# First group of two chunk pairs ahead of the second group in both MLP up stages, own memory for its tiles, weight block sums two pairs late

## The chip, the core and the metric

The kernel runs on one core of a Trainium2 chip. The core has a matrix engine (TensorE, "PE" in the profile, with its weight loads as "PEld"), a vector engine (VectorE, "DVE"), a scalar engine (ScalarE, "ACT"), GpSimd ("POOL") and a sync engine ("SP"), which here issues all transfers between HBM and the on-chip memory. Each engine works through a queue of its own in a fixed order and waits for others by semaphores. The metric is device time in microseconds (us) of one execution; lower is better.

## What is computed

The reference is a network of two layers over 256 context tokens and 1024 latent tokens of width 1024: a gated convolution mixer in the first layer, an mLSTM mixer in the second, each followed by a dense MLP with squared ReLU and a hidden width of 4096. All of it is in float32. The change touches the MLP alone:

```python
def _sqrelu_mlp(h, w1, w2):
    return jnp.square(jax.nn.relu(h @ w1)) @ w2

...
        x = x + mx[2] * _rmsnorm(yx, nw[1])
        x = x + mx[5] * _rmsnorm(_sqrelu_mlp(_modulate(_rmsnorm(x, nw[2]), mx[3], mx[4]), mlp_w1[i], mlp_w2[i]), nw[3])
```

## The kernel before, in words

**Products.** Each float32 matrix is split into a rounded part and its remainder (a cast on ACT, a subtraction on DVE), and a product is three passes over the parts. Both MLP products are done blockwise: the operands are cut into 2 x 2 blocks, and seven products of sums of blocks take the place of eight block products. The sums over token blocks are made once (`sums`, `pre_norm2`, L313 to L351), those over weight blocks for each chunk pair.

**MLP up, `mlp_up` (L484).** The hidden width makes 32 chunks of 128, taken as NQ = 16 chunk pairs. `up_weights` (L401) loads two chunks of w1 into `raw` tiles (a ring of three buffers of 4 KB, L406), makes three difference blocks (two of them into `tw` tiles, two buffers), and splits seven pieces into a ring of eight slots. `up_group` (L427) multiplies them with one group of tokens: seven products of twelve matmuls into four accumulators X, Y, Z, W, some of them filled twice, with ACT and DVE taking sums out on the way into a store tile `st` (L439, tag `st7`, seven blocks), whose last line stores it to `hid_d` in HBM (L465). There are two token groups, A0 (384 of 640 half tokens in layer 0, 256 of 512 in layer 1) and A1 (256). `down_sums` (L467) loads the two chunks of w2 that belong to a pair, makes four differences and stores them to `t_d`, which `mlp_down` reads later.

**Order around the start.** `out_proj` ends with the last token tiles; what fills A0 is done inside it, and the last two token pairs are left as two functions in `left`, each of which makes one half of A1: four steps of four transposes, two copies on ACT into a `val` tile, four sums on DVE into an `S` tile, and two splits into A1 (L326 to L351; `val` and `S` share one tag, two buffers). Before: pair 0 with A0, then `left`, then pair 0 with A1, the block sums of pair 0, then pairs 1 to 15 with A0 and A1 each and their block sums behind them; in the last pair A1 comes first.

**MLP down, `mlp_down` (L503).** Seven products one after the other, each over 16 pairs: a piece of w2 or `t_d` (`w_piece`, through `raw` and the ring) and a piece of `hid_d` (`h_piece`: loaded into `hr`, three buffers, L521; split into `hp`, four buffers, L522 and L523), both prefetched. Sums go to four quarter tiles in the pool Y.

**Memory and order.** Pools are stacks at the left and the right end of the on-chip memory, and a pool opened on bytes of a closed one waits, tile by tile, for the last user of what lay there. Before, the store tiles and `tw` lie in M0 and M on the right, M0 where the post-norm tiles T of `out_proj` were; A1 is the lowest pool on the left in the up stage, H the lowest in the down stage, and Y lies on the right. A list scheduler sets the fixed order of each queue: of the instructions that it deems ready, the one that comes first in the program.

## Time and profile before

| | |
|---|---|
| median of the runs | 2597.91 us (3 runs, 2596.24 to 2599.75) |
| profiled execution | 2592.09 us, span 2590.3 us |
| PE busy | 2489.9 us, 96% of the span |
| DVE busy | 1640.9 us, 63% |
| ACT busy | 1139.0 us, 44% |
| MLP up of layer 0 | 528.03 to 950.61 us of the span |
| MLP up of layer 1 | 1921.42 to 2269.56 us |
| mean granted PE clock | 0.986 of full speed |

One execution was recorded by the hardware profiler. Times in its rows are microseconds from the start of the span. A row of the timeline joins neighbouring instructions of one line; its bracket says how long the engine stood idle before it and what ended that. Matmul ends are modelled, so the start of the next row is the better end of a group.

### The profile page before, as it was taken

What the parts mean: (1) busy time and instruction counts of PE and PEld (TensorE: products, weight loads), DVE (VectorE), ACT (ScalarE), POOL (GpSimd) and SP (SyncE); (2) the same over time, 40 slices, a digit from 0 to 9 for tenths busy, and PEclk for the clock granted to TensorE, in tenths of its full rate; (3) what the DMA queues carried; (4) which work ended last, traced back from release to release, by engine and by line L of the source; (5) the groups of instructions that cost most, each with busy time, mean ns of one, the idle gap of its engine ahead of it and who ended that gap; (6) DMA issues with size and microseconds to landing.
All of it is one profiled execution on the core that took longest, in us unless ns stands there. A gap on an engine that the chain in (4) does not pass through costs nothing.

```text
span 2590.3 us, 38783 instructions
## 1 busy us (share of the span) xinstructions
PE 2489.9 (96%) x14520; PEld 2202.5 (85%) x14520; DVE 1640.9 (63%) x3036; ACT 1139.0 (44%) x2489; POOL 104.8 (4%) x229
## 2 busy tenths in 40 slices
PE   8999999979999999999999899999998999999998
PEld 6888887879999998888879788887778999988887
DVE  5777885676766754445863755546467877754565
ACT  6311113554454544334654434345455555544443
POOL 1000000100000000000111100000010000000010
PEclk9999999989999999999999999999998999999999
DMA  8456663426656675555751322222426777776575
GB/s 294 131 176 192 204 191 111 154 98 238 238 209 228 219 252 177 169 170 169 236 175 57 73 78 58 67 73 61 150 99 213 251 261 252 234 248 190 183 228 186
DMA packets 229631, 452.77 MB, mean 175 GB/s; under 512 B 17738, under 2 KB 109178, under 8 KB 229442
## 3 DMA queue, kind: packets, MB, share of 16 engines
q1 hardware_dynamic: 229442, 450.29, 53.5%
q8 instruction: 114, 1.87, 0.3%
q14 instruction: 75, 0.61, 0.1%
HBM read 324.68 MB, written 125.33 MB: 174 GB/s over the span
## 4 chain that ended last, share of the span: by engine, by line
PE 53%; issue 30%; DVE 7%; DMA 6%; ACT 2%; POOL 2%; SPq 0%; DVEq 0%; POOLq 0%; ACTq 0%
PE psd L528 11%; PE op L371 5%; PE psZ L429 4%; PE psW L429 4%; PE psX L429 4%; PE psv L857 3%; PE psc L129 3%; PE pso L129 3%; PE psb L129 3%; PE psu L129 3%; DMA Dm<-nm_d 3%; PE psY L429 2%; DMA mraw<-in_mod_w_dram 2%; PE psq L129 1%; POOL rstd L242 1%
## 5 line engine op out<-in xcount | busy, mean ns | idle before, releaser
L528 PE MATMUL psd<-w,hp 128*128 128x512 f32 x3024 | 705.0, 395 | 0.0
L528 PEld LDWEIGHTS psd<-w,hp 128*128 128x128 f32 x3024 | 569.1, 188 | 132.0
L523 DVE TENSOR_TENSOR hp<-hr,hp 128x512 fp32r<-128x512 f32 (+1 forms) x226 | 169.5, 752 | 254.9 <-ACT hp L522 254.5
L522 ACT CAST hp<-hr 128x512 fp32r<-128x512 f32 (+1 forms) x226 | 151.1, 669 | 325.5 <-PE psd L528 291.4
L123 DVE TENSOR_TENSOR w<-raw,w 128x512 fp32r<-128x512 f32 x384 | 261.7, 686 | 37.2 <-ACT w L122 36.9
L122 ACT CAST w<-raw 128x512 fp32r<-128x512 f32 x384 | 236.5, 617 | 94.8 <-DMA raw<-in_w_dram 29.6
L429 PE MATMUL psX<-A,w 128*128 128x256 f32 (+1 forms) x1536 | 233.4, 300 | 4.9 <-ACT st L444 3.7
L429 PE MATMUL psZ<-A,w 128*128 128x256 f32 (+1 forms) x1536 | 230.9, 298 | 0.2 <-DVE st L448 0.2
L429 PE MATMUL psW<-A,w 128*128 128x256 f32 (+1 forms) x1536 | 228.1, 296 | 0.0
L429 PEld LDWEIGHTS psX<-A,w 128*128 128x128 f32 x1536 | 216.7, 192 | 6.0 <-ACT st L444 4.0
L429 PEld LDWEIGHTS psZ<-A,w 128*128 128x128 f32 x1536 | 215.4, 190 | 0.6 <-DVE st L448 0.4
L429 PEld LDWEIGHTS psW<-A,w 128*128 128x128 f32 x1536 | 213.0, 189 | 0.2 <-DVE st L450 0.2
L371 PE MATMUL op<-w,zs 128*128 128x512 f32 x864 | 205.7, 397 | 6.5 <-ACT zs L365 4.4
L371 PEld LDWEIGHTS op<-w,zs 128*128 128x128 f32 x864 | 162.2, 190 | 43.6 <-ACT zs L365 5.4
L459 ACT ACTIVATE st<-st 128x256 f32<-128x256 f32 (+1 forms) x192 | 85.3, 444 | 249.1 <-DVE st L450 181.9
L220 DVE SCALAR_TENSOR_TENSOR macc<-mraw,sil,macc 128x1024 f32<-128x1024 f32 x112 | 140.6, 1282 | 37.4 <-DMA mraw<-in_mod_w_dram 37.0
L109 ACT CAST w<-raw 128x1024 fp32r<-128x1024 f32 (+1 forms) x73 | 75.4, 1041 | 161.7 <-PE psc L129 60.4
L110 DVE TENSOR_TENSOR w<-raw,w 128x1024 fp32r<-128x1024 f32 (+1 forms) x73 | 87.8, 1210 | 80.1 <-ACT w L109 79.0
L857 PE MATMUL psv<-w,hT 128*128 128x256 f32 (+1 forms) x960 | 133.8, 293 | 1.1 <-ACT val L270 0.9
L429 PE MATMUL psY<-A,w 128*128 128x256 f32 (+1 forms) x768 | 121.6, 305 | 12.8 <-ACT w L122 11.6
L857 PEld LDWEIGHTS psv<-w,hT 128*128 128x128 f32 x960 | 123.7, 192 | 1.9 <-ACT val L270 1.2
L429 PEld LDWEIGHTS psY<-A,w 128*128 128x128 f32 x768 | 111.2, 195 | 15.2 <-ACT w L122 12.4
(242 smaller groups left out, 3437.7 us busy)
## 6 DMA issues: line engine op xcount, KB each, us to landing
hid_d<-st SPq DMA_DIRECT2D x48, 896.0 KB, 5.8
mraw<-in_mod_w_dram SPq DMA_DIRECT2D x80, 512.0 KB, 4.0
hr<-hid_d SPq DMA_DIRECT2D x104, 320.0 KB, 4.2
raw<-in_w_dram SPq DMA_DIRECT2D x64, 512.0 KB, 4.4
rw<-in_w_dram SPq DMA_DIRECT2D x64, 512.0 KB, 5.4
raw<-t_d SPq DMA_DIRECT2D x128, 256.0 KB, 3.2
hr<-hid_d SPq DMA_DIRECT2D x122, 256.0 KB, 2.8
raw<-in_w_dram SPq DMA_DIRECT2D x96, 256.0 KB, 3.9
```

The source lines that it names most:

```text
L110: nc.vector.tensor_sub(w[1], src, w[0].bitcast(F32))
L122: nc.scalar.copy(w[:, 0], src)
L123: nc.vector.tensor_sub(w[:, 1], src, w[:, 0].bitcast(F32))
L129: nc.tensor.matmul(ps, w[a][:, k * P : (k + 1) * P], hold["hT"][:, k, b, t0 : t0 + n], start=(k == 0 and i == 0), stop=(k == KD - 1 and i ...
L220: nc.vector.scalar_tensor_tensor(ac[v], raw, s, ac[v], ALU.mult, ALU.add)
L371: nc.tensor.matmul(ps[h], zs[:, a, k, :], ws[k][b][:, h * 512 : (h + 1) * 512], start=(k == 0 and i == 0), stop=(k == KD - 1 and i == 2),)
L429: nc.tensor.matmul(ps, w[i][:, a, k * P : (k + 1) * P], A[:, PIECE[i], b, k, :], start=(first and k == 0 and j == 0), stop=(k == 3 and j = ...
L459: nc.scalar.activation(c, c, AF.Relu)
L522: nc.scalar.copy(h[:, 0], r)
L523: nc.vector.tensor_sub(h[:, 1], r, h[:, 0].bitcast(F32))
L528: nc.tensor.matmul(ps, h[:, a, o : o + P], w[:, b], start=(first and j == 0), stop=(last and j == 2))
L857: nc.tensor.matmul(ps[:, 0 : self.g], hold["hT"][:, k, a_, t * P : (t + 1) * P], self.wv[k // self.per][b_][:, k % self.per * self.g : (k ...
```

## The change

Each `mlp_up` now takes group A0 of pairs 0 and 1 first, with `left` traced between the two, then group A1 of pair 1, and then makes the pieces of pair 0 a second time for its group A1. From pair 2 on both groups follow each other, A0 first, in the last pair too. The block sums of pair q come after the weights of pair q + 2; those of the last two pairs stand at the end. The store tile of A0 lies in a pool of its own on the left (S1, S3) with one buffer, that of A1 in M with one buffer; M itself goes from two buffers to one. The difference tiles of the first two pairs come from the `raw` ring. The `val` and `S` tiles of `left` get three buffers in layer 0 and four in layer 1. In the down stage Y moves from the right to the left, below H.

```diff
--- before.py
+++ after.py
@@ -325,7 +325,7 @@

         def rest(A, c0, pl, tag, m):
             for k0 in range(0, 4, m):
-                val, S = [pl.tile([P, 4, m, P], F32, tag=tag, name=nm) for nm in ("val2", "S2")]
+                val, S = [pl.tile([P, 4, m, P], F32, tag=tag, name=nm, bufs=4 if l and m == 1 else 3) for nm in ("val2", "S2")]
                 for kk in range(m):
                     pt = tp.tile([P, 512], F32, tag="tp", name="pt2")
                     for j in range(2):
@@ -398,7 +398,7 @@

     NQ = DFF // P // 2

-    def up_weights(l, q, M):
+    def up_weights(l, q, M=None):

         raw = []
         for j in range(2):
@@ -406,7 +406,11 @@
             nc.sync.dma_start(r, w1[l, 2 * q + j])
             raw.append(r)
         (b11, b21), (b12, b22) = [(r[:, 0:512], r[:, 512:1024]) for r in raw]
-        t2, t3 = [M.tile([P, 512], F32, tag="tw", name="tw", bufs=2) for _ in range(2)]
+        if M is None:
+            tw = rawp.tile([P, 1024], F32, tag="raw", name="tw0")
+            t2, t3 = tw[:, 0:512], tw[:, 512:1024]
+        else:
+            t2, t3 = [M.tile([P, 512], F32, tag="tw", name="tw", bufs=2) for _ in range(2)]
         w = {1: piece(b11)}
         nc.vector.tensor_sub(t3, b22, b12)
         nc.vector.tensor_sub(b12, b12, b11)
@@ -420,7 +424,7 @@
         w[4] = piece(b21)
         return w

-    def up_group(l, q, w, A, n, c0, M, acc):
+    def up_group(l, q, w, A, n, c0, pl, acc):


         def prod(ps, i, first):
@@ -436,7 +440,7 @@
                     )

         bank = lambda nm: acc.tile([P, 512], F32, tag="acc", name=nm)[:, 0:n]
-        st = M.tile([P, 7, n], F32, tag="st7", name="st7")
+        st = pl.tile([P, 7, n], F32, tag="st7", name="st7", bufs=1)
         r11, r12, r22, c21, u2 = [st[:, i] for i in (0, 1, 2, 5, 6)]
         X, Y, Z, W = bank("psX"), bank("psY"), bank("psZ"), bank("psW")
         add = nc.vector.tensor_add
@@ -481,24 +485,28 @@
         nc.sync.dma_start(t_d[l, k, :, 2], b12)
         nc.sync.dma_start(t_d[l, k, :, 0:2], r[1].rearrange("p (a b) -> p a b", a=2))

-    def mlp_up(l, As, sX, left, acc):
+    def mlp_up(l, As, sX, left, S1, acc):
+

         (A0, n0), (A1, n1) = As
-        with pool("M0", bufs=1, side="right") as M:
+        w = up_weights(l, 0)
+        up_group(l, 0, w, A0, n0, 0, S1, acc)
+        w = up_weights(l, 1)
+        for f in left:
+            f(A1)
+        up_group(l, 1, w, A0, n0, 0, S1, acc)
+        sX.close()
+        with pool("M", bufs=1, side="right") as M:
+            up_group(l, 1, w, A1, n1, n0, M, acc)
             w = up_weights(l, 0, M)
-            up_group(l, 0, w, A0, n0, 0, M, acc)
-            for f in left:
-                f(A1)
-        sX.close()
-        with pool("M", bufs=2, side="right") as M:
             up_group(l, 0, w, A1, n1, n0, M, acc)
-            down_sums(l, 0, M)
-            for q in range(1, NQ):
+            for q in range(2, NQ):
                 w = up_weights(l, q, M)
-                both = [(A0, n0, 0), (A1, n1, n0)]
-                for A, n, c0 in both if q < NQ - 1 else both[::-1]:
-                    up_group(l, q, w, A, n, c0, M, acc)
-                down_sums(l, q, M)
+                down_sums(l, q - 2, M)
+                up_group(l, q, w, A0, n0, 0, S1, acc)
+                up_group(l, q, w, A1, n1, n0, M, acc)
+            down_sums(l, NQ - 2, M)
+            down_sums(l, NQ - 1, M)

     def mlp_down(l, pairs, xsrc, finish, T, H, Y, acc, G):

@@ -768,14 +776,14 @@
         sB.close()
         sT.close()
         set_ring()
-        with pool("A1", bufs=1) as pA1:
+        with pool("S1", bufs=1) as S1, pool("A1", bufs=1) as pA1:
             A1 = pA1.tile([P, 7, 2, 4, 256], F32R, name="A1")
-            mlp_up(0, ((A0, 384), (A1, 256)), sX, left, acc)
+            mlp_up(0, ((A0, 384), (A1, 256)), sX, left, S1, acc)
         sA.close()
     sH, sT = ExitStack(), ExitStack()
     new_hT(sH)
     T = sT.enter_context(pool("T1", bufs=2, side="right"))
-    with pool("H", bufs=1) as H, pool("Y", bufs=1, side="right") as Y:
+    with pool("Y", bufs=1) as Y, pool("H", bufs=1) as H:

         def finish(t, xt, tt):
             if t >= NCT:
@@ -1121,11 +1129,11 @@
     sG.close()
     sT.close()
     set_ring()
-    with pool("A3", bufs=1) as pA1:
+    with pool("S3", bufs=1) as S1, pool("A3", bufs=1) as pA1:
         A1 = pA1.tile([P, 7, 2, 4, 256], F32R, name="A3")
-        mlp_up(1, ((A0, 256), (A1, 256)), sX, left, acc)
+        mlp_up(1, ((A0, 256), (A1, 256)), sX, left, S1, acc)
     sA.close()
-    with pool("T3", bufs=2, side="right") as T, pool("H2", bufs=1) as H, pool("Y2", bufs=1, side="right") as Y:
+    with pool("T3", bufs=2, side="right") as T, pool("Y2", bufs=1) as Y, pool("H2", bufs=1) as H:

         def finish2(t, xt, tt):
             for h in range(2):
```

## Rows read from the trace of the kernel before

**Rows 1.** Timeline of PE (start, length, engine, line, tiles, count), end of layer 0's up stage
```profile
901.11 2.27 PE L429 MATMUL psX<-A,w 128*128 128x384 f32 x12
...
915.89 1.59 PE L429 MATMUL psX<-A,w 128*128 128x256 f32 x12
...
925.87 1.58 PE L429 MATMUL psX<-A,w 128*128 128x256 f32 x12
...
950.61 9.68 PE L528 MATMUL psd<-w,hp 128*128 128x512 f32 x41
```

**Rows 2.** Timeline of PE, start of layer 0's up stage
```profile
528.03 2.29 PE L429 MATMUL psX<-A,w 128*128 128x384 f32 x12
...
536.24 4.21 PE L429 MATMUL psX<-A,w 128*128 128x384 f32 x12 [3.72 <-ACT st L444]
...
551.30 1.04 PE L335 MATMUL pt<-ident,tt 128*128 128x128 f32 x8
...
604.09 2.27 PE L429 MATMUL psX<-A,w 128*128 128x384 f32 x12
```

**Rows 3.** Timeline of PE, start of layer 1's up stage
```profile
1921.42 1.61 PE L429 MATMUL psX<-A,w 128*128 128x256 f32 x12
...
1989.54 1.58 PE L429 MATMUL psX<-A,w 128*128 128x256 f32 x12
```

**Rows 4.** Waits of PE, 527 to 605 us (total us, times, longest)
```profile
PE pt L335 <- ACT val L338: 5.4, 3, 3.7
PE psY L429 <- ACT w L122: 4.7, 1, 4.7
PE psX L429 <- ACT st L444: 3.7, 1, 3.7
```

**Rows 5.** Waits of PE, 1920 to 2000 us
```profile
PE psY L429 <- ACT w L122: 6.8, 2, 5.4
PE pt L335 <- ACT val L338: 6.1, 3, 3.8
```

**Rows 6.** Busy: stretch, length, PE, PEld, DVE, ACT, POOL, PE clock, DMA, GB/s
```profile
528.00:604.00 76.00, 61.36 (x369) 58.57 (x368) 56.69 (x121) 42.13 (x89) 1.67 (x5) 0.87 0.43 146
1921.00:1990.00 69.00, 54.51 (x375) 52.29 (x374) 53.48 (x121) 40.76 (x89) 1.67 (x5) 0.83 0.43 145
```

**Rows 7.** Timeline of ACT, start and end of layer 0's up stage
```profile
535.71 0.48 ACT L444 COPY st<-psX 128x384 f32<-128x384 f32 x1 [1.73 <-DVE tt L387]
...
939.04 1.45 ACT L522 CAST hp<-hr 128x640 fp32r<-128x640 f32 x2
```

**Rows 8.** Timeline of DVE, start of the up stages of both layers
```profile
555.54 0.55 DVE L464 TENSOR_TENSOR st<-st 128x384 f32<-128x384 f32 x1
...
559.70 0.69 DVE L349 TENSOR_TENSOR A<-S,A 128x512 fp32r<-128x512 f32 x1 [0.69 <-ACT A L348]
...
562.67 0.69 DVE L349 TENSOR_TENSOR A<-S,A 128x512 fp32r<-128x512 f32 x1 [0.69 <-ACT A L348]
...
1917.93 1.89 DVE L123 TENSOR_TENSOR w<-raw,w 128x512 fp32r<-128x512 f32 x3
...
1945.84 0.42 DVE L463 TENSOR_TENSOR st<-st 128x256 f32<-128x256 f32 x1
1946.18 0.42 DVE L464 TENSOR_TENSOR st<-st 128x256 f32<-128x256 f32 x1
```

**Rows 9.** DMA: issues of the span by tile; stores of L465, 1990 to 2270 us
```profile
raw<-in_w_dram SPq DMA_DIRECT2D x64, 512.0 KB, 4.4
...
DMA to landing us min/median/max: 4.5/5.8/7.7
```

**Rows 10.** SP, end of layer 0's up stage: longest wait (925 to 945 us), issues
```profile
SPq L521 <- PE psW L429: 5.4, 1, 5.4
...
919.95 0.38 SPq L465 DMA_DIRECT2D hid_d<-st  x1
...
936.02 1.27 SPq L521 DMA_DIRECT2D hr<-hid_d  x3
```

## The prediction

> **What bounds the kernel now.** The first thing to read is TensorE's list of waits, because the change touches only the two MLP up stages. Inside the pairs TensorE runs without a pause: a group on A0 of layer 0 takes 915.89 - 901.11 = 14.78 us, a group of 256 columns 925.87 - 915.89 = 9.98 us, and the first down product (950.61) follows the last up group with no idle time in its bracket [rows 1]. So the middle of the stage can't be shortened by anything here, and what is left are its two ends.
>
> The start is where time is lost. The first four groups of layer 0 last from 528.03 to 604.09, 76.1 us [rows 2]. Their own work is 2 x 14.78 + 2 x 9.98 = 49.5 us and 32 transposes at 1.04 / 8 us each, 4.2 us [rows 1, 2]: 53.7 us, so 22.4 us are lost. In layer 1 it is 1989.54 - 1921.42 = 68.1 us against 4 x 9.98 + 4.2 = 44.1 us [rows 1, 3]: 24.0 us lost. The waits give the reasons. In layer 0 TensorE waits 5.4 us for ACT's copies of the transposes, 4.7 us for a weight split, 3.7 us for the first copy into the store tile; the other two groups are 0.7 us [rows 4]. In layer 1 it is 6.8 and 6.1 us, with 1.5 us of smaller ones [rows 5]. That makes 14.5 and 14.4 us. The rest, 7.9 and 9.6 us, is the lower clock after the pauses: twelve matmuls of 384 columns took 4.21 us at 536.24, after a pause of 3.72 us, and 2.28 us in the full stage [rows 1, 2], with a mean granted clock of 0.87 and 0.83 in the two stretches [rows 6], so part of the time was at 1.2 GHz. Layer 0 has three long pauses, so I price the clock at 7.9 / 3 = 2.6 us for each pause of three us or more.
>
> Each wait has a known cause. The copy at 535.71 had idled for DVE's L387 on the last tile [rows 7]: the store tile lay on memory of the post-norm tiles. The 4.7 us hang, as I read the code, on the split of a difference tile, whose two buffers are shared with the block sums of pair 0. The transposes wait because a step of four products has only two buffers for its val and S tiles: the last subtractions of two steps start 562.67 - 559.70 = 2.97 us apart, and in each DVE idles 0.69 us for ACT [rows 8]. VectorE itself is busy 56.7 of 76 us and 53.5 of 69 us [rows 6], so it is the next bound: what is saved in waits is saved only as far as VectorE has work to put there.
>
> **The change part by part.** *The start, layer 0.* The store tile lies in S1 and the difference tiles of the first two pairs in the raw ring, so nothing of them waits for the post-norm (what lay on S1's bytes, out_proj's ring slots for k = 4 and 5, was last read before 528), and the first group runs 528.03 to 542.8 without the 3.7 us. The 16 + 16 transposes come when it ends (in the kernel before, the second pair's eight at 551.30 also came only when a group was done [rows 2]). TensorE then has 4.2 + 14.78 us of ready work, the transposes and group (1, A0), up to 561.8. A1's path is longer: 1.0 us of transposes ahead of the first step [rows 2], eight steps, and what VectorE still owes the first group, five of nine evictions. An eviction of 256 columns occupies 1946.18 - 1945.84 = 0.34 us; at 384 columns it lasts 0.55 against 0.42 us, so I take 0.45 [rows 8]: 2.3 us. A step occupies VectorE 2.97 - 0.69 = 2.28 us. With three or four buffers the idle 0.69 can be filled by the next step; the bounds of a step are 2.28 us (all of it) and 2.97 us (none). I take 2.28, as other VectorE work is queued too and idle time is what the added buffers attack. So A1 is whole at 542.8 + 1.0 + 8 x 2.28 + 2.3 + 0.7 (last subtraction) = 565.0, and TensorE pauses 3.2 us, one clock price of 2.6. The two groups on A1 take 20.0 us. Beside them VectorE has the second set of pair 0's pieces, eleven operations at 1.89 / 3 = 0.6 us [rows 8], 6.6 us, and 9 x 0.34 = 3.1 us of evictions for every 9.98 us: it just fits, and I add 1.5 us for the lag (bounds 0 and 4, what is left of the first groups' evictions). End at 589.1 for 604.1: **15.0 us gained**.
>
> *The start, layer 1.* Group (0, A0) ends at 1931.4. Pair 1's raw tiles can be loaded when pair 0's are split, about 1922, and land 4.4 us later [rows 9]. From 1926.4 VectorE has 6.6 us of pieces, 3.1 us of evictions and 0.8 us of post-norm, done at 1936.9, beside TensorE's group. Then eight steps and 1.0 us: A1 is whole at 1956.1. TensorE has run out at 1931.4 + 4.2 + 9.98 = 1945.6, pays one clock price, then 20.0 us and 1.5 us lag: 1980.2 for 1989.5, **9.3 us gained**. Here VectorE is the bound and the earlier group only fills the wait.
>
> *Second set of pieces for pair 0.* Per layer two loads of 512 KB, seven casts, eleven VectorE operations. VectorE's 6.6 us are counted above; the casts lie on ACT, which is behind VectorE in both stretches (42.1 and 40.8 us busy [rows 6]); the loads pass on SP's queue ahead of pair 2's. If the cover of the A1 groups were gone they would cost 6.6 us per layer.
>
> *Block sums two pairs late.* The same loads, four subtractions and three stores per pair, moved on SP's queue past two pairs of weight loads and group stores; nothing reads them before the second down product. In the middle they cost nothing, as TensorE hides them there before and after; at the start they leave the difference buffers to the pieces (in the figures above); at the end two sets of sums remain instead of one. POOL has nothing moved past it.
>
> *One store tile for each group instead of two buffers.* The A0 store is issued 919.95 - 915.89 = 4.1 us after its group ends [rows 1, 10]; stores land after 4.5 to 7.7 us [rows 9], so the tile is free at 11.8 us at the latest. Its next write comes after the A1 group and one product, 9.98 + 2.11 = 12.1 us. I take 0 (bounds 0 and 2 us); a gain is excluded, since no store was waited for there. The Trainium skill speaks against this edit: "Trainium Kernel Development and Optimization", section Best Practices, asks for double buffers so that DMA overlaps compute. By the trace the other group is the second buffer; by the rule it would be the last rival below.
>
> *The end: A1 last, H above Y.* This edit has a price, and no row shows it directly. Before, A1's group came first in the last pair. Y now lies lowest on the left and H above it: in layer 0 Y takes 40 KB, so H spans 40 to 67.5 KB while A1 spans 10.5 to 66.5 KB; in layer 1 32 to 54 KB inside 7 to 63 KB. H waits for A1 whole: SP's wait before the first h load is 5.4 us on psW, the last product of A1's group, and the three loads were issued at 936.02, just as that group ended [rows 10], although hr's own bytes were last read by its first product. After the change A1's group is the very last. TensorE then has nothing until the first load lands and is cast: 939.04 + 0.73 - 936.02 = 3.75 us [rows 7, 10], and then a clock price of 2.6: 6.35 us a layer, **12.7 us lost** in both (bounds 3.4 + 1.9 with a smaller tile and the one row's clock loss, and 6 + 3.2 if the loads share the DMA engines with the sums).
>
> *Sum.* 15.0 + 9.3 - 12.7 = 11.6 us. The profiled execution took 2592.09 us (span 2590.3 and 1.8 around it) and would take 2580.5. It lies 5.8 us under the median of the runs, 2597.91; on that the forecast is **2586.3 us**, 0.45% faster. About 0.2%, 5.2 us, is what a measurement of this kernel can tell from no change.
>
> **Rivals.** *The hole at the end isn't there* (H placed or awaited otherwise): 2597.9 - 24.3 = 2573.6. For it: no row shows where H will lie, the KB come from the tile sizes in the code; against it stands the wait on psW.
> *The step keeps its chain.* If a step stays at 2.97 us, A1 comes 5.5 us later in each layer, the start gains 9.5 + 3.8 us and the end takes 12.7 of it: 2597.3, no change. For it: each step still goes ACT, VectorE, ACT, VectorE, with one more buffer in layer 0; against it: the idle 0.69 us is small and other work is there.
> *Slower: the first h loads queue behind the last block sums.* All of them go through SP's one queue, which itself waits (the 5.4 us above). If the h load stands there behind a store of pair 15's sums, it waits for their load, four subtractions and the store before it: 2.4 us and, priced as a raw tile of the same 512 KB, 4.4 us twice [rows 9], up to 11.2 us more a layer, 2586.3 + 22.4 = 2608.7. It decides from 5.8 us of extra wait a layer. For it: two sums are left for the end; against it: SP issued the h loads ahead of other work at 936.02.
> *Slower: the single store tile.* A store that lands later than 8 us delays the group's first copy, and from some 4 us more (three products of 1.4 us) TensorE too; each us beyond is paid in 28 pairs: 2614 for one. The rows' longest is 7.7.
>
> **How the numbers follow.** Forecast 0.50, own range 2580 to 2594 by the bounds; no hole 0.12; chain kept 0.20; sums in the way 0.12; single store tile 0.06. The range must reach down to the case without a hole and up over the kept chain, 2573 to 2600, and leaves out 0.18. Faster by over 0.2%: nine tenths of the forecast, the case without a hole and a little of the kept chain, 0.60. Slower: the last two and a little of the kept chain, 0.20. Within: 0.20.
>
> **What would show it.** Right: no wait of the first group for its copy; steps of A1 some 2.3 us apart; four groups done 61 us after the first psX in layer 0 and 59 us in layer 1; a TensorE pause of 3 to 5 us before the first psd matmul in both layers, with the h load on SP waiting for psW and the clock low after it. Wrong: TensorE seamless into psd, steps still 3 us apart, copies of psX waiting for a store, or new pauses in the middle of a stage.

## The result and the profile after

The changed kernel takes **2578.51 us** (median of 4 runs, 2577.89 to 2583.12) against 2597.07 us for the kernel before, run beside it: a ratio of **0.9926**, 95% interval 0.9909 to 0.9942. A second set of runs on another chip gave 0.9936 (0.9924 to 0.9948). That is 18.6 us by medians; 2586.3 us and 11.6 us were forecast. The profiled execution took 2577.89 us with a span of 2576.1 us; the forecast on that scale was 2580.5. The two spans, 2590.3 and 2576.1 us, differ by only 14.2 us: the profiled execution of the kernel before lies 5.0 us under its median, and the first up stage of the kernel after began 2.6 us later (530.65 against 528.03 us). That start lies between 526.9 and 531.9 us over all runs told of here, and nothing below is read from it.

The gain sits where the forecast had it, at the two ends of the two MLP up stages. The timeline of PE after, at the end of both up stages (columns as in [rows 1]):

```profile
934.83 1.58 PE L433 MATMUL psW<-A,w 128*128 128x256 f32 x12
940.87 49.44 PE L536 MATMUL psd<-w,hp 128*128 128x512 f32 x200 [4.45 <-ACT hp L530]
...
2242.80 1.58 PE L433 MATMUL psW<-A,w 128*128 128x256 f32 x12
2248.35 5.49 PE L536 MATMUL psd<-w,hp 128*128 128x512 f32 x12 [3.97 <-ACT hp L530]
2256.19 44.11 PE L536 MATMUL psd<-w,hp 128*128 128x512 f32 x182 [2.35 <-ACT hp L530]
```

Four lengths describe the run. The *work* of an up stage goes from the start of its first psX row to the end of its last psW row: in layer 0 it began at 530.65, so 934.83 + 1.58 - 530.65 = 405.8 us (422.7 before), in layer 1 at 1913.40, so 331.0 us (348.3 before). That is **17.0 and 17.3 us gained** where 15.0 and 9.3 were forecast. The *hole* is the time from there to the first psd row: 4.5 us in layer 0 and 4.0 us in layer 1, where before psd followed at once [rows 1]. The *middle* goes from layer 0's first psd row to layer 1's first psX row: 1913.40 - 940.87 = 972.5 us (970.8 before). The *tail* is the rest of the span: 2576.1 - 2248.35 = 327.8 us (320.7 before); it holds the second pause of 2.35 us in the rows above. All experiments below are read by these four. Each comes from one profiled execution, and two profiles of the changed kernel differ by up to 1.5 us in one of them, so differences of that size carry little by themselves.

At the start, the waits of PE from 528 to 605 us, to be set against [rows 4]:

```profile
PE pt L335 <- ACT val L338: 2.1, 1, 2.1
PE psX L433 <- ACT st L448: 0.6, 1, 0.6
PE psX L433 <- DVE w L123: 0.4, 1, 0.4
PE psZ L433 <- DVE st L452: 0.2, 1, 0.2
```

The first copy of 3.7 us and the weight split of 4.7 us are gone, and the transposes wait 2.1 instead of 5.4 us. In layer 1, 1912 to 1985 us, against [rows 5]:

```profile
PE pt L335 <- ACT val L338: 3.5, 3, 1.4
PE psX L433 <- ACT st L448: 1.1, 1, 1.1
```

The busy times of two stretches of the same lengths (columns as in [rows 6]) show that VectorE does more in the same time, 62.7 and 62.9 us instead of 56.7 and 53.5, and that the granted clock is nearly whole:

```profile
530.00:606.00 76.00, 72.72 (x469) 70.97 (x468) 62.69 (x136) 49.23 (x106) 1.88 (x5) 0.98 0.50 172
1913.00:1982.00 69.00, 64.30 (x514) 62.58 (x513) 62.87 (x146) 49.68 (x112) 2.08 (x5) 0.98 0.55 187
```

At the end of layer 0, SP's wait (925 to 945 us) and its issues, against [rows 10], show what the hole waits for: the h loads stand waiting for psW, the last product ends at 936.41 and they go out at 936.45, ahead of the store of that last group.

```profile
SPq L529 <- PE psW L433: 4.0, 1, 4.0
...
936.45 1.27 SPq L529 DMA_DIRECT2D hr<-hid_d  x3
939.44 0.37 SPq L469 DMA_DIRECT2D hid_d<-st  x1
```

In layer 1 one h load goes out at 2244.41, and the second stands behind stores of the block sums that are left; that these make the second pause is tested below (e4 and e5):

```profile
2244.41 0.32 SPq L529 DMA_DIRECT2D hr<-hid_d  x1
...
2251.06 0.32 SPq L484 DMA_DIRECT2D t_d<-t  x1
2251.79 0.32 SPq L485 DMA_DIRECT2D t_d<-rw  x1
2252.16 0.43 SPq L529 DMA_DIRECT2D hr<-hid_d  x1
```

### The profile page after: what moved, and what is told of

Same layout as the page of the kernel before. It is cut to its first block, busy times and chain, and to the rows that moved or that the text cites. A ratio compares the mean times of both kernels' runs of the same rounds, so it can differ in the third digit from the quotient of the medians.

```text
span 2576.1 us, 38825 instructions
## 1 busy us (share of the span) xinstructions
PE 2488.1 (97%) x14520; PEld 2199.3 (85%) x14520; DVE 1651.6 (64%) x3058; ACT 1143.7 (44%) x2503; POOL 107.0 (4%) x229
## 4 chain that ended last, share of the span: by engine, by line
PE 53%; issue 30%; DVE 6%; DMA 6%; ACT 3%; POOL 2%; DVEq 0%; POOLq 0%; SPq 0%; ACTq 0%
PE psd L536 12%; PE op L371 5%; PE psZ L433 4%; PE psW L433 4%; PE psX L433 4%; PE psv L865 3%; PE psc L129 3%; PE pso L129 3%; DMA Dm<-nm_d 3%; PE psb L129 3%; PE psu L129 3%; PE psY L433 2%; DMA mraw<-in_mod_w_dram 2%; PE psq L129 1%; DVE macc L220 1%
## 5 line engine op out<-in xcount | busy, mean ns | idle before, releaser
L123 DVE TENSOR_TENSOR w<-raw,w 128x512 fp32r<-128x512 f32 x394 | 268.2, 685 | 40.9 <-ACT w L122 40.8
L122 ACT CAST w<-raw 128x512 fp32r<-128x512 f32 x394 | 242.5, 617 | 105.6 <-DMA raw<-in_w_dram 37.1
L433 PE MATMUL psY<-A,w 128*128 128x256 f32 (+1 forms) x768 | 116.0, 297 | 0.0
L129 PE MATMUL psc<-hT,w 128*128 128x512 f32 (+1 forms) x576 | 115.2, 352 | 0.6 <-DVE hT L279 0.4
```

The source lines that it names most:

```text
L122: nc.scalar.copy(w[:, 0], src)
L123: nc.vector.tensor_sub(w[:, 1], src, w[:, 0].bitcast(F32))
L129: nc.tensor.matmul(ps, w[a][:, k * P : (k + 1) * P], hold["hT"][:, k, b, t0 : t0 + n], start=(k == 0 and i == 0), stop=(k == KD - 1 and i ...
L433: nc.tensor.matmul(ps, w[i][:, a, k * P : (k + 1) * P], A[:, PIECE[i], b, k, :], start=(first and k == 0 and j == 0), stop=(k == 3 and j = ...
```

## The experiments

The theory after the result: the start gains because three things that each kept TensorE waiting go together (the copies into reused memory, the steps that make A1, the weight splits behind the block sums), with a second group on A0 as work for the meantime; the end loses because the first products of the down stage need memory that A1 holds to its last read, and loads that stand in SP's queue. The rivals: one of the parts does it alone; or the hole comes from the block sums that are left over. The table has every run that is told of below; "work", "hole", "middle" and "tail" are in us, from the profiled execution, as defined above; the ratio is to the kernel before on the same chip.

| kernel | work 0 | hole 0 | middle | work 1 | hole 1 | tail | median | ratio (interval) |
|---|---|---|---|---|---|---|---|---|
| before | 422.7 | 0 | 970.8 | 348.3 | 0 | 320.7 | 2597.07 | 1 |
| after | 405.8 | 4.5 | 972.5 | 331.0 | 4.0 | 327.8 | 2578.51 | 0.9926 (0.9909 to 0.9942) |
| e0_after | 404.3 | 5.0 | 971.7 | 330.9 | 4.2 | 329.1 | 2578.05 | 0.9936 (0.9924 to 0.9948) |
| e1_a1_first | 406.2 | 0 | 975.3 | 332.4 | 0 | 325.7 | 2568.98 | 0.9907 (0.9884 to 0.9929) |
| e2_h_lowest | 405.6 | 5.6 | 977.9 | 331.0 | 5.3 | 327.9 | 2582.95 | 0.9959 (0.9944 to 0.9974) |
| e3_whole_a1 | 407.7 | 4.7 | 973.2 | 335.2 | 4.9 | 328.5 | 2582.89 | 0.9960 (0.9944 to 0.9975) |
| e4_no_last_sums | 405.5 | 3.8 | 972.3 | 331.0 | 4.6 | 323.5 | 2569.44 | 0.9902 (0.9872 to 0.9931) |
| e5_a1_first_sums_done | 406.1 | 0 | 971.8 | 332.5 | 0 | 321.1 | 2561.96 | 0.9869 (0.9851 to 0.9887) |
| e6_two_buffers | 408.9 | 5.0 | 975.0 | 336.6 | 5.5 | 326.8 | 2587.75 | 0.9980 (0.9968 to 0.9992) |
| e7_one_group_ahead | 413.1 | 5.1 | 976.6 | 333.2 | 5.0 | 327.2 | 2591.00 | 0.9981 (0.9966 to 0.9995) |
| e8_sums_not_late | 417.2 | 3.7 | 977.2 | 342.5 | 4.8 | 324.8 | 2594.76 | 0.9996 (0.9982 to 1.0011) |
| e9_one_pair_late | 407.1 | 4.3 | 970.4 | 333.4 | 5.8 | 323.9 | 2576.91 | 0.9930 (0.9916 to 0.9943) |
| e10_hole_alone | 421.9 | 12.3 | 977.4 | 348.9 | 4.9 | 323.1 | 2618.14 | 1.0088 (1.0075 to 1.0102) |
| e11_own_memory | 424.1 | 13.9 | 975.8 | 351.0 | 12.1 | 323.4 | 2627.46 | 1.0128 (1.0114 to 1.0142) |

In the middle, behind the first few products, the kernels differ only in where Y and H lie and in the last pieces that e4 reads, yet it varies from 970.4 to 977.9 us. What lies in it beyond the slower products behind a hole is not explained here, so a part is judged by its own column first.

### What the end costs

**A1 first in the last pair**, as it was before the change, on the changed kernel:

```
-                up_group(l, q, w, A0, n0, 0, S1, acc)
-                up_group(l, q, w, A1, n1, n0, M, acc)
+                both = [(A0, n0, 0, S1), (A1, n1, n0, M)]
+                for A, n, c0, pl in both if q < NQ - 1 else both[::-1]:
+                    up_group(l, q, w, A, n, c0, pl, acc)
```

> The changed kernel, with A1's group ahead of A0's in the last pair of each layer. If the pause before the first down product is H waiting for A1's last reader, it goes in both layers: the h loads are issued some 15 us (layer 0) and 10 us (layer 1) before the up stage ends, and 6.3 us of layer 0 and up to 11 us of layer 1 come back, less 0 to 3 us a layer, since two A1 groups then follow each other on one store tile: 2578.5 - 17 + 0 to 6, that is 2561 to 2567 us. If the pause comes from the last two block sums ahead of the h loads in SP's queue, the h loads stay late and at most the psW part is saved: about 2570 us or more, with a pause of some 3 us left.

The first psd row follows the last group without a pause in both layers (hole 0 and 0), with the same two sets of block sums left over, so the hole comes from A1's group being last. One pause stays, in layer 1. The timeline of PE, end of layer 0 and of layer 1:

```profile
934.17 16.03 PE L537 MATMUL psd<-w,hp 128*128 128x512 f32 x68
...
2241.67 2.96 PE L537 MATMUL psd<-w,hp 128*128 128x512 f32 x12
2247.19 52.98 PE L537 MATMUL psd<-w,hp 128*128 128x512 f32 x219 [2.56 <-ACT hp L531]
```

The second pause of the changed kernel (2.35 us) is still there, so it has a cause of its own. The time fell by less than expected: by the ratios 4.9 to 7.5 us, with 11 to 17 expected, and the interval overlaps that of the changed kernel. The holes of 4.5 and 4.0 us are gone, the work is 0.4 and 1.4 us more, and the middle of this profile is 2.8 us longer, which is not explained.

**Without the last two block sums** (their pieces are read from w2 instead; the sums of pairs 14 and 15 of each layer are left out):

```
-            down_sums(l, NQ - 2, M)
-            down_sums(l, NQ - 1, M)
```

> The changed kernel without the last two block sums of each layer; the pieces of w2 that would read them take a block of w2 itself. If layer 1's second pause (2.35 us) and the late second h load are SP's queue holding the loads and stores of those sums ahead of them, the second pause goes and the first stays near 4 us: 3 to 5 us faster than the changed kernel, 2573 to 2575 us. If the second pause is the transfer time of the h loads themselves, it stays: 2578 us.

In layer 1 only the first pause is left (4.57 us), and the tail falls from 327.8 to 323.5 us: 4.3 us, as the queue theory said. The sums that are left over make the second pause.

```profile
2247.35 52.92 PE L534 MATMUL psd<-w,hp 128*128 128x512 f32 x220 [4.57 <-ACT hp L528]
```

By the ratios this kernel is 6.2 to 8.8 us faster than the changed one, more than the 3 to 5 expected, but its four runs lie 11 us apart and the intervals overlap; the reading rests on the pause and the tail.

**Both taken away**, with all sums kept: A1 first as above, and the sums caught up inside the loop.

```
-                down_sums(l, q - 2, M)
+                down_sums(l, q - 2 + (q > 6) + (q > 10), M)
+                if q in (6, 10):
+                    down_sums(l, q - 1 + (q > 6), M)
...
-            down_sums(l, NQ - 2, M)
-            down_sums(l, NQ - 1, M)
```

> Two edits on the changed kernel: A1's group ahead of A0's in the last pair, and the block sums caught up inside the loop (a second set in pairs 6 and 10), so that none is left behind the last group. Theory, the hole at the end has two parts (h waits for A1's last read, and the later h loads stand in SP's queue behind the last two block sums): with both taken away the first down product follows without a pause in both layers, no second pause comes in layer 1, and the time is 14 to 18 us under the changed kernel, some 4 to 5 us under the one with A1 first alone. Rival, the second pause has another cause (the cast on ACT, the DMA engines): it stays, and the time is that of A1 first alone, 9 to 12 us under the changed kernel.

Both holes and the second pause are gone; PE goes from the last group of layer 1 into a psd row that runs on unbroken:

```profile
2239.61 1.60 PE L433 MATMUL psW<-A,w 128*128 128x256 f32 x12
2241.05 59.18 PE L537 MATMUL psd<-w,hp 128*128 128x512 f32 x254
```

The tail is 321.1 us, that of the kernel before. With 2561.96 us it is the fastest kernel of this study, and its interval lies wholly under those of the changed kernel. The ratios, each to the kernel before on its own chip, differ by 0.9926 - 0.9869 = 0.0057, or 0.0067 from the second set of runs: 14.8 to 17.4 us, as expected (14 to 18). So A1's place and the sums left over together account for the price of the end.

**H lowest again** (Y back on the right; the same in layer 1):

```
-    with pool("Y", bufs=1) as Y, pool("H", bufs=1) as H:
+    with pool("H", bufs=1) as H, pool("Y", bufs=1, side="right") as Y:
```

> The changed kernel with Y back on the right and H lowest on the left, so that hr (7.5 and 6 KB) lies on the store tile of A0 alone (10.5 and 7 KB) and only hp still lies on A1. If the waits go by what lies on the bytes, the h loads are issued before A1's last group ends, as soon as A0's last store has landed, and the pause shrinks from 4.45 and 3.97 us to the cast of about 1 to 1.5 us: 5 to 10 us faster than the changed kernel, 2569 to 2574 us. If the place of H is not what holds the loads, or if A0's last store lands too late, the pauses stay and the time stays at 2578.5 us or rises.

A miss of the theory; the other case that was named, A0's last store landing too late, came true. The holes grew, to 5.6 and 5.3 us. SP's waits at the end of layer 0 (930 to 945 us) name what the h loads waited for:

```profile
SPq L529 <- DMA hid_d<-st: 4.3, 1, 4.3
```

They waited for a store to land, no longer for psW. In the changed kernel S1 is the lowest pool, so H in the lowest place lies on the store tile of the A0 groups and waits until the last of their stores has landed. Putting Y lowest is what keeps H off that tile; it is worth about a microsecond a layer of hole here, and far more when A0's group is the last one (e11 below). By the ratios this kernel is 6.0 to 8.6 us slower than the changed one; the part beyond the holes lies in the middle (977.9 us) and is not explained.

**The end alone, on the kernel before:** A0 ahead of A1 in the last pair too, Y lowest, H above it (in layer 1 too).

```
-                for A, n, c0 in both if q < NQ - 1 else both[::-1]:
+                for A, n, c0 in both:
...
-    with pool("H", bufs=1) as H, pool("Y", bufs=1, side="right") as Y:
+    with pool("Y", bufs=1) as Y, pool("H", bufs=1) as H:
```

> The kernel before with the end of the change alone: A0's group ahead of A1's in the last pair too, Y lowest and H above it; the start, the buffers and the block sums stay as they were. Theory as predicted, the first h load waits for A1's last product: 6.35 us a layer, 12.7 us slower than the kernel before (layer 1 up to 10 us if its second h load stands behind the one set of sums: 16). Rival, the hole in the changed kernel comes from the two sets of sums that are left: then 4 us or less.

22.7 us slower by medians, more than any theory gave. The hole in layer 1 is 4.9 us, but in layer 0 it is 12.3 us, and SP's issues show why:

```profile
954.16 0.38 SPq L465 DMA_DIRECT2D hid_d<-st  x1
955.36 0.33 SPq L513 DMA_DIRECT2D raw<-in_w_dram  x1
955.74 2.43 SPq L521 DMA_DIRECT2D hr<-hid_d  x3
```

The last product ended at 949.45, but here the store of that last group and a load of w2 stand in the queue ahead of the h loads, and the store goes only when VectorE's last subtraction (L464, 953.72) is done. The loads went out 6.3 us after the last product, not 0.04 us as in the changed kernel. So the length of the hole depends on when A1's memory comes free and on the place in the queue. The rival (the two sets of sums left over make it) falls: with one set left the hole is longer here, and with two left it is gone in e1. Why the fixed order of the queue came out differently was not tried.

### What the start gains

**Two buffers for `val` and `S`** again:

```
-                val, S = [pl.tile([P, 4, m, P], F32, tag=tag, name=nm, bufs=4 if l and m == 1 else 3) for nm in ("val2", "S2")]
+                val, S = [pl.tile([P, 4, m, P], F32, tag=tag, name=nm) for nm in ("val2", "S2")]
```

> The changed kernel with two buffers for the val and S tiles of the left steps, as before the change. Theory as predicted, the added buffers let VectorE fill the 0.69 us of idle time in each step: steps 2.97 us apart again, A1 complete 5.5 us later in each layer, 5 to 11 us slower (5 if only one layer pays). Rival, VectorE is the bound and has other work for the idle time (pieces of pair 1, evictions): the steps keep their distance on average, within 2 us.

The work grows by 408.9 - 405.0 = 3.9 us and 336.6 - 331.0 = 5.6 us, 405.0 and 331.0 being the means of both profiles of the changed kernel. Their sum is within the 5 to 11 us expected; the ratio of 0.9980 is 11 to 14 us above, and the difference lies in the middle (975.0) and the holes (5.0 and 5.5 us), which the buffers do not explain. The last subtraction of each step on DVE, first and last of the eight, in layer 0 and layer 1 of this kernel:

```profile
553.99 0.69 DVE L349 TENSOR_TENSOR A<-S,A 128x512 fp32r<-128x512 f32 x1 [0.68 <-ACT A L348]
...
577.24 0.69 DVE L349 TENSOR_TENSOR A<-S,A 128x512 fp32r<-128x512 f32 x1 [0.69 <-ACT A L348]
...
1937.68 0.69 DVE L349 TENSOR_TENSOR A<-S,A 128x512 fp32r<-128x512 f32 x1 [0.22 <-ACT A L348]
...
1959.58 0.69 DVE L349 TENSOR_TENSOR A<-S,A 128x512 fp32r<-128x512 f32 x1 [0.69 <-ACT A L348]
```

and of the changed kernel, layer 0 and layer 1, there with the second and third too:

```profile
553.69 0.69 DVE L349 TENSOR_TENSOR A<-S,A 128x512 fp32r<-128x512 f32 x1
...
572.19 0.69 DVE L349 TENSOR_TENSOR A<-S,A 128x512 fp32r<-128x512 f32 x1 [0.91 <-ACT A L348]
...
1931.14 0.68 DVE L349 TENSOR_TENSOR A<-S,A 128x512 fp32r<-128x512 f32 x1
...
1933.69 0.69 DVE L349 TENSOR_TENSOR A<-S,A 128x512 fp32r<-128x512 f32 x1
...
1935.57 0.69 DVE L349 TENSOR_TENSOR A<-S,A 128x512 fp32r<-128x512 f32 x1
...
1945.23 0.68 DVE L349 TENSOR_TENSOR A<-S,A 128x512 fp32r<-128x512 f32 x1
```

In layer 0 a step takes (577.24 - 553.99) / 7 = 3.32 us with two buffers and 2.64 us with three; in layer 1 it takes (1959.58 - 1937.68) / 7 = 3.13 us with two and (1945.23 - 1931.14) / 7 = 2.01 us with four. The buffers do what they were forecast to do.

**A1 used from its last quarter** (pair 1's group on A1 goes through the four inner blocks backwards, so that it starts only with the last step of A1):

```
-            for k in range(4):
+            for k in ks:
...
-            up_group(l, 1, w, A1, n1, n0, M, acc)
+            up_group(l, 1, w, A1, n1, n0, M, acc, (3, 2, 1, 0))
```

> The changed kernel with the inner loop of group (1, A1) run from the last quarter of A1 to the first, so that TensorE can start it only when A1 is whole. If the start went better than forecast because TensorE used A1 quarter by quarter while it was made, this gives back the pause I had forecast: about 2 us in layer 0 and 7.5 us in layer 1, 2588 us, with a TensorE pause of 3 us and 8 us and a low clock behind it. If it went better because the steps of A1 were shorter than priced or VectorE's lag was smaller, it changes less than 3 us: 2578 to 2581 us.

2.7 and 4.2 us more work. In the changed kernel TensorE takes A1's products a quarter at a time while the steps still run; the forecast had A1 as usable only when whole. In layer 0 the price shows as a wait of 2.6 us for A, in layer 1 as 3.2 us of psZ waiting for VectorE's sum out of the accumulator, VectorE being late there:

```profile
565.27 0.38 PE L433 MATMUL psX<-A,w 128*128 128x256 f32 x1 [2.56 <-ACT A L348]
...
1942.61 2.93 PE L433 MATMUL psZ<-A,w 128*128 128x256 f32 x12 [3.15 <-DVE st L452]
```

Layer 0 is near the 2 us expected, layer 1 well under the 7.5. The sum of 6.9 us fits the ratios, 6.2 to 8.8 us slower than the changed kernel.

**One group ahead** (pair 0's on A0 alone; pair 1's follows pair 0's A1 group, and no weights are made twice):

```
         up_group(l, 0, w, A0, n0, 0, S1, acc)
-        w = up_weights(l, 1)
         for f in left:
             f(A1)
-        up_group(l, 1, w, A0, n0, 0, S1, acc)
...
-            up_group(l, 1, w, A1, n1, n0, M, acc)
-            w = up_weights(l, 0, M)
             up_group(l, 0, w, A1, n1, n0, M, acc)
+            w = up_weights(l, 1, M)
+            up_group(l, 1, w, A0, n0, 0, S1, acc)
+            up_group(l, 1, w, A1, n1, n0, M, acc)
```

> The changed kernel with pair 0's A0 group alone ahead of A1, pair 1's behind pair 0's A1 group; no weights are made twice, and S1, the buffers of val and S, the late block sums and the placing of H stay. Theory, the second group is what fills the wait for A1: TensorE pauses again for the steps, some 16 us of steps against 14.8 (layer 0) and 10 us (layer 1) of work that is missing, less what the quarters of A1 already feed; the stage grows by 5 to 10 us in each layer, 10 to 20 us in all. Rival, the own memory, the buffers and the late sums do it and the second group only trades work: under 4 us, or faster by VectorE's 6.6 us of pieces that aren't made twice.

8.1 us more work in layer 0, inside the expected 5 to 10, but only 2.2 us in layer 1, less than expected. There the waits for the transposes' copies grow by 2.0 us alone (5.5 instead of 3.5). The short steps with four buffers and the 11 fewer VectorE operations are a likely reason, which was not tested. PE's waits from 525 to 610 us in layer 0 (7.6 us where the changed kernel has 2.1):

```profile
PE pt L335 <- ACT val L338: 7.6, 5, 2.5
```

**The block sums not late**: those of pairs 0 and 1 behind pair 0's A1 group, each later set behind its pair.

```
             up_group(l, 0, w, A1, n1, n0, M, acc)
+            down_sums(l, 0, M)
+            down_sums(l, 1, M)
             for q in range(2, NQ):
                 w = up_weights(l, q, M)
-                down_sums(l, q - 2, M)
                 up_group(l, q, w, A0, n0, 0, S1, acc)
                 up_group(l, q, w, A1, n1, n0, M, acc)
-            down_sums(l, NQ - 2, M)
-            down_sums(l, NQ - 1, M)
+                down_sums(l, q, M)
```

> The changed kernel with each pair's block sums directly behind its groups: those of pairs 0 and 1 behind pair 0's A1 group, one set left at the end. Theory, lateness relieves the start and costs at the end: 8 subtractions of 0.6 us, 4.8 us of VectorE, and a share in the difference buffers come back ahead of pair 2's pieces, 1 to 4 us a layer; at the end one set less stands ahead of layer 1's second h load, 2 us back. Sum 0 to 6 us slower. Rival, TensorE is already covered by two A1 groups by then: the start pays nothing, and the time is 2 to 4 us less.

A miss, and the largest single price: 12.2 us and 11.5 us more work, the whole gain gone (2594.76 against 2594.66 us for the kernel before). The profiled execution was one of the slower ones, 4.3 us above its median; by the ratios the price is 15.6 to 18.2 us, where 0 to 6 were expected. PE stands here in layer 0 (and 8.5 us in the same place in layer 1):

```profile
599.05 1.01 PE L433 MATMUL psY<-A,w 128*128 128x384 f32 x2 [7.88 <-ACT w L122]
```

The chain behind it can be read off SP and DVE of the same kernel:

```profile
584.43 0.32 SPq L486 DMA_DIRECT2D t_d<-rw  x1
...
585.91 1.86 SPq L476 DMA_DIRECT2D rw<-in_w_dram  x2
...
593.44 0.69 DVE L480 TENSOR_TENSOR t<-rw 128x512 f32<-128x512 f32 x1 [0.50 <-DMA rw<-in_w_dram]
594.05 0.68 DVE L415 TENSOR_TENSOR tw<-raw 128x512 f32<-128x512 f32 x1
```

Pair 1's w2 chunks can be loaded (585.91) only when pair 0's differences are on their way out of the same two tiles (584.43). Its first difference (L480) waits for them until 593.44, and pair 2's first weight difference (L415) stands behind it in DVE's fixed order: 594.05, which is 66.8 us after the first psX of this run (527.28). The changed kernel has it at 585.36, 54.7 us after its first psX (530.65), 12.1 us earlier:

```profile
585.36 0.68 DVE L415 TENSOR_TENSOR tw<-raw 128x512 f32<-128x512 f32 x1
```

**One pair late**: only pair 0's sums ahead of pair 2's weights.

```
             up_group(l, 0, w, A1, n1, n0, M, acc)
+            down_sums(l, 0, M)
             for q in range(2, NQ):
                 w = up_weights(l, q, M)
-                down_sums(l, q - 2, M)
+                down_sums(l, q - 1, M)
...
-            down_sums(l, NQ - 2, M)
```

> The changed kernel with the block sums one pair late instead of two: those of pair 0 behind pair 0's A1 group, ahead of pair 2's weights, each later set between a pair's weights and its groups, one set left at the end. Theory, the wait of 7.9 us that came with the sums of pairs 0 and 1 back to back hangs on the second set (its load waits for the first set's stores, and it shares the difference buffers with pair 2's pieces); one set alone was done at 584 in that run, before pair 2's pieces, so the start stays as in the changed kernel (within 2 us a layer) and the end gains 2 to 4 us in layer 1. Rival, any set ahead of pair 2's pieces brings TensorE's wait for a weight split back: 5 to 12 us more a layer.

The theory holds about as far as it goes: no wait of psY for a weight split comes back, the work grows by 2.1 and 2.4 us, a little over the 2 us allowed, and the tail gains 3.9 us (327.8 to 323.9). By medians it is the changed kernel (0.9930 against 0.9936 on the same chip). So the sums have to be out of the way of pair 2's weights, and one pair of lateness does nearly all of that.

**The own memory alone**, on the kernel before: A0's store tile in S1 and pair 0's difference tiles in the raw ring, single store tiles; one group ahead, two buffers, sums as before, A1 first in the last pair, H lowest.

> The kernel before with the own memory alone: the A0 groups' store tile in S1 (one, not two), pair 0's first difference tiles in the raw ring, one store tile for A1; one group ahead, two buffers for val and S, block sums as before, A1 first in the last pair, H as before. Theory, it takes the one wait of 3.7 us and one clock price of 2.6 us at the start of layer 0 and nothing in layer 1, whose first copy didn't wait long: 4 to 7 us faster than the kernel before. Rival, what is saved there is lost in the later waits for VectorE's pieces, or single store tiles cost in the middle: within 2 us, or slower.

32 us slower, where 4 to 7 us faster were expected; the rival, that what is saved at the start is lost in later waits, came true there, and most of the rest is the end. Two things show. At the start nothing is gained: the work is 424.1 us against 422.7, and 351.0 against 348.3 in layer 1. In layer 0 TensorE only reaches the next wait sooner. PE's waits from 530 to 610 us, to be read beside [rows 4]:

```profile
PE pt L335 <- ACT val L338: 10.2, 5, 3.7
PE psY L433 <- ACT w L122: 4.7, 1, 4.7
```

The 3.7 us for the first copy are gone and the wait for the transposes' copies is 4.8 us longer. At the end the holes are 13.9 and 12.1 us: H is lowest, on S1, and here A0's group is the last, so the first h load waits for that group's store to land (wait of SP, 955 to 970 us):

```profile
SPq L525 <- DMA hid_d<-st: 5.0, 1, 5.0
```

That is the mechanism of e2 with the last group on the wrong tile. It belongs to this mixture of edits and not to the own memory as such, so the 32 us are no price of that part; the work of the two up stages is.

## Why the prediction was right, and where it was not

**Right in direction, range and place; short by 7 us.** 2578.5 us lies inside 2573 to 2600, and 18.6 us were gained where 11.6 were forecast. Of the marks named there, the first group without a wait for its copy, the steps, the pause before psd with the h load waiting for psW, and the low clock behind it came. Of the marks for a wrong forecast one came in small: the copies of psX idled for a store twice, 1.0 us in all. The total is nearer than its parts: the starts gave 34.3 us where 24.3 were forecast, the ends took 17.2 where 12.7 were forecast, and the two errors partly cancel, which is luck.

**Start of layer 0, 15.0 forecast, 17.0 measured.** The first group ran without its wait and the steps came 2.64 us apart, between the two bounds of 2.28 and 2.97. The 3.2 us pause for A1 did not come as such, since TensorE took A1 by quarters. With that taken back, in e3, the work is 407.7 us and the gain 422.7 - 407.7 = 15.0 us, the forecast's own number; the quarters are what lies above it, 2.0 to 2.7 us.

**Start of layer 1, 9.3 forecast, 17.3 measured: the mis-sized term.** Two steps of the working failed. "A1 is whole at 1956.1" was made the moment from which A1 could be used; by quarters is 4.2 us better (e3). And a step was put at 2.28 us of VectorE at least; with four buffers it took 2.01 us, and two steps with nothing else between them start 1935.57 - 1933.69 = 1.88 us apart (rows of e6 above). So 2.28 us was more than a step's own work: 8 x 0.27 = 2.2 us, worked out from the step times and not from a run of its own. Together 6.4 of the 8.0 us; the rest was not taken apart. The statement that VectorE is the bound there held: 62.9 of 69 us busy.

**What the parts are worth.** The forecast summed the parts; the runs show that they hold each other up. Taken back one at a time (work in layer 0 and 1): the second buffers 3.9 and 5.6 us, the second group 8.1 and 2.2, the late sums 12.2 and 11.5. These sum to 24.2 us in layer 0, where the whole change gains 17.0, and the own memory alone gains nothing. The reading that fits this is that each removes one of several waits that end close to one another, so that one that is left takes the place of the one removed; e11 shows it for the own memory, where the transposes' wait grew by 4.8 us for the 3.7 us saved. "Block sums two pairs late" stood in the prediction as a half-sentence, with its gain put into the start; its mechanism (the shared difference buffers and VectorE's queue) was named rightly and its weight was not.

**The end of layer 0: 6.35 us forecast.** The pause was 4.5 us (3.75 forecast), and the middle, where the slow products behind it fall, 1.7 us longer than before: 6.2 us. The middle varies by more than that; by the granted clock (last section) the slow stretch cost 2.7 to 3.0 us, 7.2 to 7.5 us in all. The h loads did wait for psW, as said. The agreement owes something to the order of one queue: in e10, the same end on the kernel before, the loads stood behind a store and the hole was 12.3 us.

**The end of layer 1: 6.35 us forecast, 11.0 measured** (4.0 us of hole and 7.0 us of longer tail). Here the rival of the h loads queued behind the last block sums came true in one layer: 2252.16 for the second load, a second pause of 2.35 us, and 4.3 us back when the last sums were left out (e4). The prediction had it as a case of 0.12 beside the forecast; it should have been a part of the price. The upper bound of 6 + 3.2 us was given there without a row, and 11.0 us lies above it.

**One store tile for each group: 0 forecast.** The costliest groups of the page after (busy us, mean ns, idle us before them) have psX waiting for the copy into the store tile for 1.7 us in all 64 groups of both layers, 0.6 and 1.1 of it at the two starts (rows above):

```profile
L433 PE MATMUL psX<-A,w 128*128 128x256 f32 (+1 forms) x1536 | 230.0, 298 | 2.2 <-ACT st L448 1.7
```

So no pair in the middle pays. The rule weighed there, double buffers so that transfers overlap compute (the Trainium skill, "Trainium Kernel Development and Optimization", section Best Practices), does not disagree with this once the other group's tile is counted as the second buffer.

## What to carry to other kernels

When several waits end close together, removing one can show nothing, as the own memory alone did, and leaving one can cost most of the gain, as the block sums did; so price a part by taking it back from the finished change. Before a stage's last group is chosen, ask whose memory the next stage's first loads lie on and which stores stand ahead of them in the same queue: here the right answer to both (A1 first, no sums left over) was worth some 15 to 17 us on top of the change. Of side work with its own load and store, ask what stands behind it in the order of the engine that does it.

## What the runs showed of the hardware

The granted clock behind a pause could be read directly. After the pause of 4.45 us in layer 0 of the changed kernel (stretch, us, busy times of PE, PEld, DVE, ACT, POOL, granted clock, DMA share, GB/s):

```profile
934.00:938.00 4.00, 2.42 (x21) 2.21 (x19) 1.04 (x3) 2.31 (x6) 0.00 (x0) 1.00 1.06 393
938.00:942.00 4.00, 1.13 (x3) 0.77 (x4) 3.77 (x8) 1.77 (x3) 0.00 (x0) 0.75 1.01 357
942.00:946.00 4.00, 4.00 (x11) 3.13 (x11) 2.35 (x4) 0.41 (x1) 0.00 (x0) 0.50 1.06 374
946.00:950.00 4.00, 4.00 (x17) 3.18 (x17) 0.05 (x1) 0.81 (x2) 0.00 (x0) 0.90 0.96 302
```

TensorE was idle from 936.4 to 940.9, the clock was at 0.50 (1.2 GHz) from 942 to 946 while it worked without a break, and back at 0.90 in the next four microseconds. The two pauses of layer 1, 3.97 and 2.35 us, left five such stretches, 2244 to 2264, at 0.91, 0.50, 0.74, 0.69 and 0.88. By these rows the slow stretch of layer 0 cost between 0.25 x 1.13 and 0.5 x 1.13 us in the second, 0.5 x 4 in the third and 0.1 x 4 in the fourth, 2.7 to 3.0 us, where the forecast took 2.6 for a pause.

The forecast counted a clock price only behind pauses of three us or more. The start of layer 0 shows one behind a shorter wait: TensorE stood for 2.11 us up to 550.34 (the transposes' wait above), and the next stretch has a mean clock of 0.61:

```profile
550.00:554.00 4.00, 3.66 (x16) 3.57 (x17) 4.00 (x12) 2.85 (x6) 0.00 (x0) 0.61 0.28 101
```

In layer 1, behind waits of 1.43, 0.75 and 1.33 us, 1936 to 1940 has 0.58. Taken as before, that is 0.39 x 3.66 = 1.4 us in layer 0.
